# A hybrid decoder layer on one core: three fills ahead of the first attention scores, compressed turns placed later, FFN tiles at fixed homes, tables and gate weights issued later

## The chip, the core and the metric

The kernel runs on one core of a Trainium2 chip. TensorE (PE) multiplies matrices into PSUM, where eight banks of 128 x 512 f32 words hold results; VectorE (DVE), ScalarE (ACT) and GpSimd (POOL) move and change data between PSUM and the on-chip memory SBUF; SyncE (SP) starts most of the DMA transfers. Each engine runs its own instructions in the order in which the program lists them, and waits on semaphores for the others. The metric is the device time of one execution in microseconds.

## The reference

One layer over a sequence of 512 tokens and 1024 channels, all in f32:

```python
h = rmsnorm(x, norm_mix_pre);  z = h @ w_in            # 1024 -> all projections
y_rnn  = rg_lru(causal_conv(xr)) * gelu(gr)            # recurrent branch
kc_c, vc_c = compress(kc), compress(vc)                # MLPs over blocks of 32 tokens
o = g0 * attn(q, kc_c, vc_c) + g1 * attn(q, k_sel, v_sel) + g2 * attn(q, k_win, v_win)
y = sigmoid(gm_rnn) * y_rnn + sigmoid(gm_attn) * o
x = x + rmsnorm(y @ w_out, norm_mix_post)
gate, up = split(rmsnorm(x, norm_ffn_pre) @ ffn_w_gate_up)
x = x + rmsnorm((silu(gate) * up) @ ffn_w_down, norm_ffn_post)
x = x + sigmoid(x @ ple_w_gate + ple_b_gate) * (p @ ple_w_proj)
```

There are 16 query heads in 4 key groups, 64 channels per head. The attention has three branches: over compressed keys (31 blocks), over selected blocks (with 8 blocks and a choice of up to 16, all are selected) and over a window of 512 tokens. Scores carry a bias that falls with distance (ALiBi).

## The kernel before, in words

**Arithmetic.** A product in full precision is three matmuls: each f32 operand is split into a high part and a low part (hi = rounded copy, lo = value - hi), and PE sums hi·hi, hi·lo and lo·hi. So weights that arrive by DMA (`raw`) are cast by ScalarE (`wh`) and subtracted by VectorE (`wl`), and activations that leave PSUM take the same two steps (`aTh` and `aTl`, `PT`, `pc`).

**Stages.** Norm and the value projections come first (up to about 40 us of the profile), then the recurrent branch and the compress MLPs (to 180), the attention (to 468), the output projection and the second norm (to 530), the FFN's gate and up products in 22 column blocks (to 748), its down product (to 860), and the gated embedding, here the tail (to 924).

**The attention's order.** The 16 heads go in 8 pairs, each in two halves of the queries, `run(p, 0, ...)` and `run(p, 1, ...)`. The order of PE's work in a run is a string, in which a letter is a step and a digit is a number of fills. S makes a block of scores (`scores`; VectorE evicts it with the bias at L837, ScalarE takes the exponential at L840). T is a turn: it transposes probabilities (`turn_step`, PE L99) and splits them into hi and lo (`PT`, ScalarE L922, VectorE L923). M multiplies them with the values. X, Y and Z are the compressed branch of the group after this one: its scores, its softmax (which ends on POOL, L888) and its turn, four transposes and the split `pc` (ScalarE L902, VectorE L904). C multiplies `pc` with the compressed values. Y's last steps scale by the gates. A fill is one step of the other projections that the layer needs (three matmuls, one eighth of the inputs of a 128 x 512 block); it keeps PE at work while the others evict. All fills come from one list, so a fill moved ahead is the same work earlier. Ahead of the first run stand the first pair's own scores, with fills between them in the numbers of `PRO`; the first group's X, Y and Z stand there too. PSUM banks are shared by name: two each for `mm` (fills), `sc` (scores) and `tr` (turns), one each for `pv` and `mq` (products).

**Keys.** The keys of a group are copied to the other half of the partitions by a DMA from POOL's queue (L750), `KS<-KS`; the first scores need them.

**Tables.** POOL builds the distance tables `toep` and `ctab` (iota and a triangular select) and clears `KC`, `Vz` and `vct`. `issue_after(x)` puts what is issued inside it behind instruction x in the program's order. `last["pow"]` is the latest power -1/2 that POOL took for a norm.

**FFN and tail.** The pool `ff` gives tiles by tag in the order of their first use, in memory that other stages have left; a tile that lies on such memory waits for its last reader. In the tail `ple_gate_load` loads 512 KB of gate weights and splits them on ScalarE (L1209) and VectorE (L1210); it runs four times for each half of the columns. `to_T` transposes x into `aTh`/`aTl` (L243, L244), the operand of the tail's product. L1380 to L1383 add the gate's bias, take the sigmoid, multiply and add.

## Time and profile before

| | |
|---|---|
| time, median of 3 runs | 924.7 us (924.44 to 926.46) |
| the profiled execution | 926.09 us, span 924.3 us |
| granted PE clock | 0.999 of full speed |
| PE busy | 903.7 us, 98% of the span |
| VectorE busy | 617.5 us, 67% |
| ScalarE busy | 491.5 us, 53% |
| POOL busy | 128.2 us, 14% |
| chain that ended last | PE 82%, VectorE 9%, ScalarE 4%, DMA 3% |

An engine's busy time is the sum over its instructions, so the rest of the span is time in which it stood still. The chain is the work that ended last, followed back from the last instruction to what released each step. In the timeline a start is a time from the start of the span; consecutive equal instructions stand in one row. The ends of matmuls are modelled, so a hole between two of them is read better from the two starts.

### The profile page before, as it was taken

The page shows a single profiled execution, that of the slowest core. Times are in us where ns is not written, and L with a number is a line of the kernel's source. Part 1 is how long each engine was busy: PE and PEld are TensorE (multiplying, and loading weights), DVE is VectorE, ACT ScalarE, POOL GpSimd, SP SyncE. Part 2 cuts the span into 40 slices and gives each one's busy share as a digit, 9 for nine tenths or more (in the row PEclk, how much of TensorE's full clock was granted, in tenths as well). Part 3 has the DMA queues.
Part 4 walks back from the last instruction along what each step waited for, and adds up shares of the span by engine and source line. Part 5 has one row for each costly group of instructions (what it writes and reads, how often), then busy time and mean ns, then how long its engine had stood idle before and what let it go on. Part 6 is the DMA issues. An engine that isn't in the chain of part 4 may idle for free.

```text
span 924.3 us, 12453 instructions
## 1 busy us (share of the span) xinstructions
PE 903.7 (98%) x4493; PEld 745.3 (81%) x4493; DVE 617.5 (67%) x1205; ACT 491.5 (53%) x898; POOL 128.2 (14%) x211
## 2 busy tenths in 40 slices
PE   7999999999999999999999999999999999999997
PEld 6978888867878878888888988888888888877786
DVE  6657886967788788886857444434333478898932
ACT  6468868656667667666744322223222245465600
POOL 3001202122243213233303000000000000000100
PEclk9999999999999999999999999999999999999999
DMA  9334345462123111201055123333333345626401
GB/s 298 87 91 114 101 118 147 99 106 66 50 60 78 46 47 46 69 30 62 27 200 160 55 83 91 102 104 91 92 104 101 91 138 186 200 93 224 151 35 46
DMA packets 124206, 94.58 MB, mean 102 GB/s; under 512 B 6168, under 2 KB 107376, under 8 KB 124144
## 3 DMA queue, kind: packets, MB, share of 16 engines
q1 hardware_dynamic: 122976, 91.68, 33.6%
q0 software_dynamic: 1152, 2.10, 1.5%
q8 instruction: 35, 0.57, 0.3%
q14 instruction: 27, 0.22, 0.1%
q10 hardware_dynamic: 16, 0.00, 0.0%
HBM read 89.58 MB, written 2.10 MB: 99 GB/s over the span
## 4 chain that ended last, share of the span: by engine, by line
PE 82%; DVE 9%; ACT 4%; DMA 3%; issue 2%; POOL 0%; SPq 0%; POOLq 0%; ACTq 0%; DVEq 0%
PE mm L96 42%; PE sc L96 24%; PE mq L96 5%; PE tr L96 4%; PE tr L99 4%; PE pv L96 4%; DVE wl L158 1%; DVE PT L923 1%; DMA x<-in_x_dram 1%; DMA KS<-KS 1%; DMA raw<-in_ple_w_gate_dram 1%; DVE aTl L1210 1%; DVE e L837 1%; ACT e L840 1%; DVE T L1222 1%
## 5 line engine op out<-in xcount | busy, mean ns | idle before, releaser
L96 PE MATMUL mm<-aTh,wh 128*128 128x512 f32 (+1 forms) x536 | 211.6, 395 | 0.6 <-ACT st L1157 0.6
L96 PE MATMUL mm<-aTl,wh 128*128 128x512 f32 (+1 forms) x536 | 206.1, 384 | 0.1
L96 PE MATMUL mm<-aTh,wl 128*128 128x512 f32 (+1 forms) x536 | 206.1, 384 | 0.0
L96 PEld LDWEIGHTS mm<-aTh,wl 128*128 128x128 f32 x536 | 100.7, 188 | 20.7
L96 PEld LDWEIGHTS mm<-aTh,wh 128*128 128x128 f32 x536 | 100.9, 188 | 20.2 <-issue 3.4
L84 ACT CAST wh<-raw 128x1024 fp32r<-128x1024 f32 x43 | 45.3, 1054 | 134.4 <-PE mm L96 58.3
L96 PEld LDWEIGHTS mm<-aTl,wh 128*128 128x128 f32 x536 | 101.0, 188 | 16.4 <-DVE aTl L244 0.5
L852 POOL TENSOR_SCALAR e<-e,sm 128x128 f32<-128x128 f32 (+3 forms) x128 | 79.2, 635 | 158.2 <-DVE sm L848 120.0
L85 DVE TENSOR_TENSOR wl<-raw,wh 128x1024 fp32r<-128x1024 f32 x43 | 52.6, 1224 | 67.3 <-ACT wh L84 62.7
L158 DVE TENSOR_TENSOR wl<-raw,wh 128x1024 fp32r<-128x1024 f32 x59 | 73.2, 1244 | 28.9 <-ACT wh L157 24.3
L840 ACT ACTIVATE e<-e,mn 128x128 f32<-128x128 f32 (+3 forms) x128 | 71.5, 560 | 31.3 <-DVE mn L837 20.4
L96 PE MATMUL sc<-aTh,wl 128*128 128x512 f32 (+1 forms) x208 | 79.3, 381 | 0.5 <-DVE wl L158 0.5
L96 PE MATMUL sc<-aTh,wh 128*128 128x512 f32 (+1 forms) x208 | 79.3, 381 | 0.0
L96 PE MATMUL sc<-aTl,wh 128*128 128x512 f32 (+1 forms) x208 | 79.2, 381 | 0.0
L157 ACT CAST wh<-raw 128x1024 fp32r<-128x1024 f32 x59 | 61.6, 1048 | 25.6 <-PE mm L96 20.9
L837 DVE CUSTOM_DVE_ANT_0 e<-sc,toep 128x128 f32<-128x128 f32 (+3 forms) x128 | 59.4, 482 | 19.2 <-PE sc L96 18.6
L923 DVE TENSOR_TENSOR PT<-tr,PT 128x512 fp32r<-128x512 f32 x96 | 56.6, 595 | 14.0 <-ACT PT L922 13.2
L922 ACT CAST PT<-tr 128x512 fp32r<-128x512 f32 x96 | 47.9, 512 | 24.9 <-PE tr L99 20.9
L1043 POOL TENSOR_TENSOR ss<-ss,ss 128x1 f32<-128x1 f32 x8 | 4.9, 615 | 388.0 <-ACT junk L1031 388.0
L96 PE MATMUL sc<-KS,QS 128*128 128x512 f32 (+2 forms) x192 | 54.3, 365 | 2.8 <-DMA KS<-KS 1.9
L99 PE MATMUL tr<-ident,e 128*128 128x128 f32 x320 | 48.5, 272 | 0.0
L99 PEld LDWEIGHTS tr<-ident,e 128*128 128x128 f32 x320 | 39.9, 140 | 8.8
(365 smaller groups left out, 1747.2 us busy)
## 6 DMA issues: line engine op xcount, KB each, us to landing
raw<-in_w_in_dram SPq DMA_DIRECT2D x48, 512.0 KB, 3.8
raw<-in_ffn_w_gate_up_dram SPq DMA_DIRECT2D x44, 512.0 KB, 3.8
raw<-in_ffn_w_down_dram SPq DMA_DIRECT2D x30, 512.0 KB, 4.3
raw<-in_ple_w_gate_dram SPq DMA_DIRECT2D x8, 512.0 KB, 4.1
x<-in_x_dram SPq DMA_DIRECT2D x7, 512.0 KB, 8.4
raw<-in_w_out_dram SPq DMA_DIRECT2D x6, 512.0 KB
raw<-in_cmp_k_w_dram SPq DMA_DIRECT2D x4, 512.0 KB, 3.7
raw<-in_cmp_v_w_dram SPq DMA_DIRECT2D x4, 512.0 KB, 3.9
```

What stands on the lines that cost most here:

```text
L84: nc.scalar.copy(h, raw)
L85: nc.vector.tensor_sub(l, raw, f32(h))
L96: return pe(nc.tensor.matmul(*args, **kw))
L99: return pe(nc.tensor.transpose(*args))
L157: nc.scalar.copy(h, RAW[n])
L158: nc.vector.tensor_sub(l, RAW[n], f32(h))
L837: nc.vector.tensor_tensor_reduce(e[:, br, :], src, toep[:, 384 - 128 * i:S], SLOPE[h], BIG, op0=OP.add, op1=OP.min, accum_out=mn[:, u, br: ...
L840: tt(nc.scalar.activation(e[:, br, :], e[:, br, :], AF.Exp, scale=-1.0, bias=mn[:, u, br:br + 1], accum_out=sm[:, u, br:br + 1]))
L852: nc.gpsimd.tensor_scalar(ev, ev, sm[:, v, br:br + 1], 1.0, op0=OP.mult, op1=OP.mult)
L922: nc.scalar.copy(P[:, 0, :2 * n], pt[:, :2 * n])
L923: nc.vector.tensor_sub(P[:, 1, :2 * n], pt[:, :2 * n], f32(P[:, 0, :2 * n]))
L1210: nc.vector.tensor_sub(l, x, f32(h))
```

## The change

Five edits. (a) `PRO` goes from 22 fills ahead of the first scores to 25, with one and two fills fewer at two later places, and the first group's turn moves from ahead of the first run into it (`FIRST`, behind the seventh score step). (b) In `ODD`, the order of the second half of pairs 1, 3 and 5, the turn Z moves past two products and the two fills between them. (c) Ahead of the FFN the tags of `ff` are each asked for once in a fixed order; these tiles are never written, they only decide the addresses. (d) POOL's tables and clears are issued behind the last power of the first norm, not behind the first one. (e) The gate weights of the second half are issued behind the last `aTh` and `aTl` of the transposes that stand inside the tail's second product.

```diff
--- before.py
+++ after.py
@@ -26,10 +26,11 @@
 
 
 HALF0 = "S T S 1 S 2 S T 1 S 2 M S T 1 S T 1 S M M 1 M C 3"
+FIRST = "S T S 1 S 2 S T 1 S 2 M S T 1 S Z T 1 S M M 1 M C 3"
 EVEN = "1 T S T 1 C S M T 1 M T 1 S M T T 1 M 1 S T 1 M T 1 M 1 M 3 M"
-ODD = "T T X 1 S M T C S 1 Y M S 1 T T M 1 S T M 1 T 2 T M Z M 2 M 1 M 1"
+ODD = "T T X 1 S M T C S 1 Y M S 1 T T M 1 S T M 1 T 2 T M M 2 M Z 1 M 1"
 LAST = "T O O T 1 C 1 O 1 M O T T O O O M 2 M M T W 4 T 2 M T M 1 T 1 M 1 M"
-PRO = (22, 5, 0, 2, 1, 10)
+PRO = (25, 4, 0, 2, 1, 8)
 TK = (1, 7, 1)
 TV = (12, 7, 8, 11)
 VP = ()
@@ -395,7 +396,6 @@
     tp(pg[:, :KT], g_rows, ident[:KT, :KT])
     kept(nc.vector.tensor_copy(g_col, pg[:, :KT]))
     xn = norm1_halves(x0)
-    pow0 = last["pow"].ins
     keep_warm(6)
     with tc.issue_after(last["xn"].ins):
         vw_first(0, 2, "a")
@@ -460,7 +460,7 @@
 
 
     late_pool = ctx.enter_context(ExitStack())
-    late_pool.enter_context(tc.issue_after(pow0))
+    late_pool.enter_context(tc.issue_after(last["pow"].ins))
     nc.gpsimd.iota(toep, pattern=[[-1, S]], base=384, channel_multiplier=1,
                    allow_small_or_imprecise_dtypes=True)
     nc.gpsimd.affine_select(toep, toep, pattern=[[-1, S]], base=384, channel_multiplier=1,
@@ -505,9 +505,10 @@
     e2 = e2_stack.enter_context(tc.tile_pool(name="e2", bufs=2, reuse_waits="tile"))
 
 
-    nc.gpsimd.memset(KC, 0.0)
-    nc.gpsimd.memset(f32(Vz), 0.0)
-    nc.gpsimd.memset(vct, 0.0)
+    with tc.issue_after(last["pow"].ins):
+        nc.gpsimd.memset(KC, 0.0)
+        nc.gpsimd.memset(f32(Vz), 0.0)
+        nc.gpsimd.memset(vct, 0.0)
     w2src = [a[n_][0].rearrange("(k p) d -> p k d", p=128) for n_ in ("cmp_k_w2", "cmp_v_w2")]
     for u in range(2):
         nc.sync.dma_start(w2k[:, :, u, :], w2src[0])
@@ -969,7 +970,7 @@
         g = p // 2 + 1
         do = {"S": lambda: scores(*next(ss)), "T": lambda: turn_step(p, half, next(ts)),
               "M": lambda: pv_step(p, half, next(ms)), "C": lambda: pv_cmp(p, half), "O": lambda: y_split(next(ys)),
-              "W": lambda: split_out(), "X": lambda: cmp_scores(g), "Y": lambda: cmp_soft(g), "Z": lambda: cmp_turn(g)}
+              "W": lambda: split_out(), "X": lambda: cmp_scores(g), "Y": lambda: cmp_soft(g), "Z": lambda: cmp_turn(g if half else 0)}
         for c in order.replace(" ", ""):
             if c.isdigit():
                 fill(int(c))
@@ -993,9 +994,8 @@
     fill(PRO[4])
     cmp_soft(0)
     fill(PRO[5])
-    cmp_turn(0)
     for p in range(KT - 1):
-        run(p, 0, HALF0)
+        run(p, 0, HALF0 if p else FIRST)
         run(p, 1, (EVEN, ODD)[p % 2])
     p = KT - 1
     run(p, 0, HALF0)
@@ -1187,6 +1187,14 @@
     lateb_stack.close()
     wo_stack.close()
     ff = ctx.enter_context(tc.tile_pool(name="ff", bufs=1, reuse_waits="tile"))
+
+    ff.tile([128, 2, S], F32, tag="st", name=nm("home"), bufs=2)
+    for j in range(NJ2):
+        if j % 2 == 0:
+            n = len(BLK[j // 2])
+            ff.tile([128, n, 4, HS], F32, tag=f"r{j // 2}", name=nm("home"))
+            ff.tile([128, n, 2, HS], F32, tag=f"a{j // 2}", name=nm("home"))
+        ff.tile([128, 2, 2, HS], F32, tag=f"s{j}", name=nm("home"))
     for f in range(2):
         gu_act(f, *first[f][1])
     for f in range(2, NF):
@@ -1363,8 +1371,9 @@
     for ch in range(2):
         for i, t in enumerate(ORDER):
             if ch == 0 and i == 2:
-                for k2 in range(4):
-                    ple_gate_load(1, k2)
+                with tc.issue_after(last["Th"].ins), tc.issue_after(last["Tl"].ins):
+                    for k2 in range(4):
+                        ple_gate_load(1, k2)
             tl = slice(t * 128, (t + 1) * 128)
             pj = bank("tr")
             three(pj, [(pT[0][:, k, tl], pT[1][:, k, tl], WP[ch][0][:, k], WP[ch][1][:, k]) for k in range(2)])
```

**PE in the first run.** `tr<-ident,c` is the compressed turn, `tr<-ident,e` a turn of probabilities, `sc` scores, `mm` a fill. Before, the turn stands between the last fill and the run's first scores:

```order
L96 MATMUL mm_2034<-aTh,wl_1893 128x512
L99 MATMUL tr_2060<-ident,c_2004 128x128 x4
L96 MATMUL sc_2074<-KS_1781,QS_1877 128x384 x2
L99 MATMUL tr_2079<-ident,e_1907 128x128
L99 MATMUL tr_2079<-ident,e_1956 128x128
L99 MATMUL tr_2079<-ident,e_1939 128x128
L99 MATMUL tr_2079<-ident,e_1981 128x128
L96 MATMUL sc_2087<-KS_1781,QS_1877 128x384 x2
```

Now, between the seventh score step of the run and the fourth turn:

```order
L97 MATMUL mm_2099<-aTh,wh_1939 128x512
L97 MATMUL mm_2099<-aTl,wh_1939 128x512
L97 MATMUL mm_2099<-aTh,wl_1940 128x512
L97 MATMUL sc_2169<-KS_1781,QS_1879 128x512 x2
L100 MATMUL tr_2174<-ident,c_2010 128x128 x4
L100 MATMUL tr_2184<-ident,e_1966 128x128
L100 MATMUL tr_2184<-ident,e_1987 128x128
L97 MATMUL mm_2099<-aTh,wh_1939 128x512
```

The turn has moved past seven score steps, three turns, one product and the fills between them. (The line numbers of the changed kernel are higher by one here, and by eight to nine in the tail, since lines were added ahead.)

**PE at the end of pair 1.** `mq<-PT` is a product. Before, the turn (`c_2658`) stands between two products:

```order
L99 MATMUL tr_2761<-ident,e_2490 128x128
L99 MATMUL tr_2761<-ident,e_2525 128x128
L96 MATMUL mq_2586<-PT_2700,V 128x512 x2
L99 MATMUL tr_2769<-ident,c_2658 128x128 x4
L96 MATMUL mq_2586<-PT_2728,V 128x512 x2
```

Now it stands two products and two fills later:

```order
L97 MATMUL mm_2754<-aTh,wl_2482 128x512
L97 MATMUL mq_2586<-PT_2749,V 128x512 x2
L100 MATMUL tr_2783<-ident,c_2658 128x128 x4
L97 MATMUL mm_2754<-aTh,wh_2481 128x512
L97 MATMUL mm_2754<-aTl,wh_2481 128x512
L97 MATMUL mm_2754<-aTh,wl_2482 128x512
L97 MATMUL mq_2586<-PT_2764,V 128x2x128 x2
```

Pairs 3 and 5 have the same order.

**VectorE where the tail begins.** `wg` is the low part of a gate weight, `aTl` the low part of the transposed x, `z` the gate, `x` the residual. Before, a weight split stands ahead of the last norm's x, and others between the `aTl`:

```order
L1210 TENSOR_TENSOR wg_7928<-raw_7925,wg_7927 128x1024
L1047 SCALAR_TENSOR_TENSOR x_5026<-C_7560,rstd_7816,x_5026 128x512
L1047 SCALAR_TENSOR_TENSOR x_5026<-U_7214,rstd_7816,x_5026 128x512
L1380 TENSOR_TENSOR z_7853<-mm_7828,b_g 128x512
L1210 TENSOR_TENSOR wg_7934<-raw_7931,wg_7933 128x1024
L244 TENSOR_TENSOR aTl<-sc_7870,aTh 128x4x128
L1210 TENSOR_TENSOR wg_7940<-raw_7937,wg_7939 128x1024
L1382 TENSOR_TENSOR z_7853<-z_7853,tr_7821 128x512
L244 TENSOR_TENSOR aTl<-sc_7877,aTh 128x4x128
L1383 TENSOR_TENSOR z_7853<-z_7853,x_5027 128x512
L244 TENSOR_TENSOR aTl<-sc_7896,aTh 128x4x128
```

Now:

```order
L1047 SCALAR_TENSOR_TENSOR x_5026<-C_7584,rstd_7840,x_5026 128x512
L1047 SCALAR_TENSOR_TENSOR x_5026<-U_7238,rstd_7840,x_5026 128x512
L1389 TENSOR_TENSOR z_7877<-mm_7852,b_g 128x512
L1391 TENSOR_TENSOR z_7877<-z_7877,tr_7845 128x512
L245 TENSOR_TENSOR aTl<-sc_7894,aTh 128x4x128
L1392 TENSOR_TENSOR z_7877<-z_7877,x_5027 128x512
L245 TENSOR_TENSOR aTl<-sc_7901,aTh 128x4x128
L245 TENSOR_TENSOR aTl<-sc_7920,aTh 128x4x128
L245 TENSOR_TENSOR aTl<-sc_7927,aTh 128x4x128
L1218 TENSOR_TENSOR wg_7952<-raw_7949,wg_7951 128x1024
```

The weight splits stand behind all four `aTl`, and the multiply of `z` by the projection (L1391) now stands ahead of the first `aTl`. On SP the last gate weight load now stands behind the first store of the output.

## Rows read from the trace of the kernel before

**Rows 1.** The list of what PE waits for, summed over the span. Columns: engine, line and tile that wait, what they wait for, then us in total, number of times, longest one.

```profile
PE tr L99 <- POOL c L888: 2.1, 3, 0.8
PE sc L96 <- DMA KS<-KS: 1.9, 1, 1.9
PE tr L99 <- DVE sm L848: 1.6, 1, 1.6
PE sc L99 <- DVE aTl L244: 1.6, 1, 1.6
```

**Rows 2.** The timeline of PE, first head pair, from the last fill before the first scores to the end of the first turn's run. Columns here and in the groups that follow: start and duration in us, engine, line, operation, output<-inputs, shape, count of instructions, and in brackets the idle time before and what ended it.

```profile
191.30 0.39 PE L96 MATMUL mm<-aTh,wl 128*128 128x512 f32 x1
193.62 0.47 PE L96 MATMUL sc<-KS,QS 128*128 128x256 f32 x2 [1.93 <-DMA KS<-KS]
...
208.93 0.39 PE L96 MATMUL mm<-aTh,wl 128*128 128x512 f32 x1
210.12 0.66 PE L99 MATMUL tr<-ident,c 128*128 128x128 f32 x4 [0.81 <-POOL c L888]
210.54 0.60 PE L96 MATMUL sc<-KS,QS 128*128 128x384 f32 x2
...
214.72 0.62 PE L96 MATMUL sc<-KS,QS 128*128 128x384 f32 x2 [0.37 <-DVE mn L837]
...
216.74 0.73 PE L96 MATMUL sc<-KS,QS 128*128 128x512 f32 x2 [0.48 <-DVE mn L837]
...
226.54 0.39 PE L96 MATMUL mm<-aTh,wh 128*128 128x512 f32 x1
```

**Rows 3.** The chain of work that ended last, the one step of it that is the DMA which copies the keys to the other half of the partitions. Columns: start, duration, what.

```profile
185.29 8.19 DMA KS<-KS
```

**Rows 4.** The timelines of POOL and VectorE in the first head pair: the scaling of the compressed probabilities, the first eviction of scores of the run, the split of the third turn's probabilities, and the last work of the run.

```profile
209.02 1.05 POOL L888 TENSOR_TENSOR c<-c,csm 128x512 f32<-128x512 f32 x1 [1.27 <-DVE csm L886]
211.17 0.56 DVE L837 CUSTOM_DVE_ANT_0 e<-sc,toep 128x384 f32<-128x384 f32 x1 [2.30 <-PE sc L96]
...
220.88 0.69 DVE L923 TENSOR_TENSOR PT<-tr,PT 128x512 fp32r<-128x512 f32 x1 [0.28 <-ACT PT L922]
...
228.17 0.85 DVE L953 TENSOR_TENSOR att<-pv,pvt 64x256 f32<-64x256 f32 x2
```

**Rows 5.** The timelines of PE, ScalarE and VectorE around the compressed turn at the end of head pair 1 and the start of pair 2.

```profile
272.60 0.66 PE L99 MATMUL tr<-ident,c 128*128 128x128 f32 x4 [1.61 <-DVE sm L848]
...
278.86 0.51 PE L96 MATMUL sc<-KS,QS 128*128 128x384 f32 x2
273.29 1.17 ACT L902 CAST pc<-tr 64x512 fp32r<-64x512 f32 x2 [1.04 <-PE tr L99]
274.49 1.39 DVE L904 TENSOR_TENSOR pc<-tr,pc 64x512 fp32r<-64x512 f32 x2 [0.46 <-ACT pc L902]
277.14 0.85 DVE L953 TENSOR_TENSOR att<-mq,pvt 64x256 f32<-64x256 f32 x2 [1.25 <-ACT pvt L951]
278.02 0.56 DVE L837 CUSTOM_DVE_ANT_0 e<-sc,toep 128x384 f32<-128x384 f32 x1
```

**Rows 6.** The same at the end of pair 3 and the start of pair 4 (PE twice, VectorE's first eviction).

```profile
337.41 0.66 PE L99 MATMUL tr<-ident,c 128*128 128x128 f32 x4 [0.67 <-POOL c L888]
...
343.67 0.51 PE L96 MATMUL sc<-KS,QS 128*128 128x384 f32 x2
342.85 0.56 DVE L837 CUSTOM_DVE_ANT_0 e<-sc,toep 128x384 f32<-128x384 f32 x1
```

**Rows 7.** The timelines of ScalarE and PE at the first silu of the FFN.

```profile
528.18 1.28 ACT L1157 ACT_TABLE_LOAD   x1
529.96 1.09 ACT L1157 ACTIVATE st<-mm 128x512 f32<-128x512 f32 x2 [0.49 <-PE sc L96]
530.61 0.50 PE L96 MATMUL mm<-aTh,wh 128*128 128x512 f32 x1 [0.57 <-ACT st L1157]
```

**Rows 8.** The timelines of POOL, ScalarE, VectorE and PE where the tail begins, and PE's first product with the gate weights of the second half of the columns (the last row).

```profile
863.87 0.55 POOL L231 TENSOR_TENSOR rstd<-rstd,mhalf 128x1 f32<-128x1 f32 x1 [0.70 <-DVE rstd L230]
866.61 1.46 POOL L231 TENSOR_TENSOR rstd<-rstd,mhalf 128x1 f32<-128x1 f32 x1 [0.70 <-DVE rstd L230]
870.20 1.28 ACT L1381 ACT_TABLE_LOAD   x1 [0.56 <-DVE z L1380]
873.50 0.68 DVE L244 TENSOR_TENSOR aTl<-sc,aTh 128x512 fp32r<-128x512 f32 x1
872.09 0.60 PE L99 MATMUL sc<-ident,x 128*128 128x128 f32 x4
874.24 0.66 PE L99 MATMUL sc<-ident,x 128*128 128x128 f32 x4 [1.56 <-DVE aTl L244]
...
892.20 0.63 PE L96 MATMUL mm<-wg,aTh 128*128 128x512 f32 x2
```

**Rows 9.** VectorE at the start of the kernel, and the step of the chain that is the load of the third tile of x.

```profile
6.38 0.77 DVE L322 TENSOR_SCALAR xn<-x,rstd 128x512 f32<-128x512 f32 x1 [0.74 <-POOL rstd L320]
...
7.14 0.47 DVE L322 TENSOR_SCALAR xn<-x,rstd 128x512 f32<-128x512 f32 x1
...
20.09 2.47 DVE L335 SCALAR_TENSOR_TENSOR xn<-x,rstd,gpre 128x1024 f32<-128x1024 f32 x2
7.62 8.49 DMA x<-in_x_dram
```

## The prediction

> **What bounds the kernel now.** I read the page first for the shares, then the list of what TensorE (PE) waits for, then the chain of waits, and last the timeline of the five places that the change touches. The shares are in the table above: PE is busy 98% of the span, at a granted clock of 0.999, so there is neither a clock to win nor an engine to relieve. What can be won is the time in which PE stands still, about 20.6 us (span less busy time), and it is scattered: the longest entries of the list are 1 to 2 us each, and each has its own releaser [rows 1]. The reader should see in that list that three of the five parts of the change stand where its entries come from: the wait for the keys' DMA (1.9) and one of the three for POOL's L888 (2.1) in the first pair, the other two of these and the one for L848 (1.6) at the turns of pairs 1, 3 and 5, and the wait for L244 (1.6) at the tail. The FFN's homes stand at a shorter wait of 0.57 [rows 7], the tables beside the first norm. The number of matmuls doesn't change. So the whole question is, wait by wait, what is late next.
>
> **First pair: three more fills, turn inside.** Before, the last fill starts at 191.30; the first scores follow at 193.62 after 1.93 of waiting [rows 2], because the shifted keys' DMA, started at 185.29, takes 8.19 us and lands at 193.48 [rows 3]. A fill (three matmuls of 512 columns) is the 0.69 us by which such matmuls follow each other in the rows before 226.54 (three starts 0.23 apart). Three fills are 3 x 0.69 = 2.07 us; they end at 191.53 + 2.07 = 193.60, and the scores can start at 193.62 as before. The three come out of the stretch behind (5 + 10 becomes 4 + 8), so PE's work up to the pair is 2.07 shorter there. The turn (four transposes, 0.42 us until the next matmul) leaves its place at 210.12, and with it the hole in front of it, from 208.93 + 0.23 = 209.16 to 210.12, which is 0.96 by starts (0.81 in the row, whose matmul ends are modelled). The first turn's run, at 210.54 before, then starts at 210.54 - 2.07 - 0.42 - 0.96 = 207.1. From there to the fill at 226.54 it took 16.0 us, of which two score steps lost 0.37 and 0.48 by their rows; a wait in a row is 0.15 short of the hole between starts (0.81 against 0.96 at the turn), so 1.15 together. The work without these is 14.85, and it now contains the turn's 0.42. Two new holes: the turn takes one of the two transpose banks, so the probability turn behind it gets the bank of the turn two fills earlier and must wait until VectorE has split that one (before at 220.88, 0.69 long [rows 4]; that turn would now come 4.2 earlier on PE, while VectorE, which waited only once for PE on the way, comes some 3.6 earlier); I put 0.5 on it and 0.1 on the product after it. The end is 207.1 + 14.85 + 0.42 + 0.6 = 222.97 against 226.54: **3.6 us**. The operand is there in time: POOL's L888 ended at 209.02 + 1.05 = 210.07, and by program order PE reaches the turn only after seven score steps and three other turns, more than 9 us behind the start of the run. The price is VectorE's: the splits of the compressed probabilities (1.39, behind ScalarE's 1.17; the same two lines as in [rows 5]) leave the start of the pair, where they held the first two score evictions up, and stand at its end. VectorE's last work of the run ended at 228.17 + 0.85 = 229.0, 2.5 after PE; the same sum of work from a start 3.5 us earlier ends near 225.1, so it doesn't become the bound. If it does, only the first 2.0 stay; if neither new hole comes, 4.3. Range 2.0 to 4.3.
>
> **Turns two products later (pairs 1, 3, 5).** The moved turn passes a product (0.46, two matmuls 0.23 apart), two fills (1.38) and a product (0.46): 2.3 us of PE's work. The waits were 1.61, 0.67 [rows 5, 6] and 0.66 (the rest of the 2.1 in rows 1 beside the first pair's 0.81), so all three go. But the splits behind the turn come later too, and they stand in ScalarE's and VectorE's queues ahead of the first evictions of the next pair, for which PE's third score step waits. Pair 1: turn at 272.60 - 1.61 + 2.30 = 273.29, ScalarE 1.17 to 274.5, with the queue ahead of it 275.15, VectorE 1.39 to 276.5, the output eviction (277.14 before, 0.85) behind it, so the next pair's first L837 starts at 277.24 and not 278.02, ends 0.56 later, and the third scores start at 277.80 and not at 278.86 [rows 5]: gain 1.06 of 1.61. Pair 3: by the same walk the splits end near 342.2, the first L837 moves from 342.85 to about 343.0, and the third scores, at 343.67 before, start at 343.6 [rows 6]: gain 0.07. Pair 5 has the order of pair 3; by the same steps 0.14. Sum **1.3 us**, with 0 (every wait reappears at the third scores) and 2.9 (none) as ends.
>
> **FFN homes.** They fix addresses only. Before, the first silu at 529.96 had waited 0.49 for a matmul, behind its table load (528.18 + 1.28 = 529.46), and PE's next bank waited 0.57 for it [rows 7]. If the first activation tile no longer lies on the up weights that PE still reads, the silu starts at 529.46 and PE's wait of 0.57 shrinks to about 0.1: **0.5 us**; ends 0 (the table load ends no earlier) and 0.6.
>
> **Tail.** The last transposes wait 1.56 for VectorE's L244 [rows 8], whose second one starts at 873.50 because three weight splits stand in VectorE's queue between the norm and it. Now the four splits stand behind all four L244. But the first L244 now stands behind the multiply by the sigmoid, which waits for a table load of 1.28 and the sigmoid itself; walking the queues, POOL's power taking 0.55, as the one before it, and not the 1.46 that it took beside the splits, then norm, z, table load (869.3), sigmoid, the first L244 starts at 871.84 and the second at 873.04. PE's step at 872.09 comes at 872.58 (0.5 later), that at 874.24 comes at 873.78: **0.5 us**. Ends: 0.5 lost (first step late, second not early) and 1.56. What was hidden before must stay so: the second half's splits now end near 883.5, with the last weight load issued behind the first output store; PE needs them at 892.20 [rows 8], so there are 8 us in hand.
>
> **Tables late.** POOL's tables no longer run beside the first norm, where VectorE's L322 took 0.77 beside them and 0.47 later [rows 9]. That lets PE begin 0.3 to 0.7 earlier, and gives nothing: the x load that starts at 7.62 and takes 8.49 sets the next norm, L335 at 20.09, and PE waits for that a second time [rows 9]. In their new place, from about 20.3 (behind the last power), the tables run beside that L335, 1.24 each. If it were slowed as L322 was (0.77/0.47, so 0.8 on 1.24), PE would lose 0.8. **0 us**, from the x load; ends -0.8 and +0.7.
>
> [...] The rows show that L322 is slower beside the index generation, which only writes. [...]
>
> **The sum.** 3.6 + 1.3 + 0.5 + 0.5 + 0 = 5.9 us off the profiled execution's 926.09, which gives 920.2. That execution was 1.4 above the median of the runs shown, 924.7; waits in it are the same events, so I take the 5.9 off the median: **918.8 us**. On this kernel about 0.2% (1.85 us) is what a measurement can tell from no change.
>
> **The rivals.**
> - *Every wait goes and nothing comes instead.* 1.93 + 0.96 + 1.15 + 2.94 + 0.57 + 1.56 = 9.1 us, 915.6 at the utmost; with any one of the new holes about 916.5. For it: each releaser is short. Against: in pairs 3 and 5 VectorE reaches the next evictions no earlier.
> - *VectorE takes the first pair over.* The moved splits meet the long evictions at the end of the first pair, PE then waits there for score banks, and of that part only the keys' wait (1.9) stays; pairs 3 and 5 give nothing, the tail nothing: 1.9 + 0.3 + 0.5 = 2.7, 922.0. For it: in rows 2 the score steps already waited for L837 twice. Against: VectorE is busy 67% of the span and had 2.30 of nothing to do before its first eviction there [rows 4].
> - *The parts cancel or do not act* (the silu bound by its table load, the new turn's place as bad as the old): within 1.85 of 924.7.
> - *Slower: the last gate weights.* The load issued behind the first output store delays the second half of the tail. It decides only if the splits end after 892.2, that is if the load lands 8 us later than I put it; for a run slower by 1.85 it would have to take the 5.9 gained as well, 8 + 5.9 + 1.85 = 15.8 us late, and then some 927. For it: one queue, a store that waits for VectorE. Against: the store's data are there at about 873.
>
> **How the numbers follow.** Forecast (4.5 to 7 us, 917.7 to 920.2) 0.60; all waits go 0.13; VectorE takes over (1.85 to 4.5 us) 0.17; cancel 0.06; slower 0.04. Range 916.4 to 922.0: it holds the forecast, the first rival up to its utmost, and the second down to its worked case, about 0.83. Faster by over 0.2%: 0.60 + 0.13 + 0.17 = 0.90; within 0.06; slower 0.04.
>
> **What would show it.** In the changed profile: no entry for the keys' DMA in PE's list, and none for L888 or L848; the first pair's last fill 3.6 earlier on the clock than 226.54; a short wait of the third score step in pairs 2, 4 and 6 for L837; the wait for L244 split into two of about 0.5 and 0.3 to 0.7; the matmul after the first silu with 0.1 of waiting; a wait of about 0.2 for L335 near 21.5 as before. Wrong would be: the start of the first pair's scores later than 193.7, a wait for L837 over 1 us inside the first pair, or PE waiting for weights at the second half of the tail.

## The result, and the profile after

The changed kernel took 920.88 us (median of 5 runs, 920.38 to 921.69) beside 925.48 us for the kernel before (5 runs, 924.44 to 929.03). The ratio is 0.9945, with a 95% interval of 0.9924 to 0.9966: faster by 0.55%, which is 3.1 to 7.0 us. The forecast was 918.8, with a range of 916.4 to 922.0. The profiled execution took 920.38 (926.09 before); its span is 918.3, 6.0 less than before.

The page's span, and the busy times of the engines:

```profile
span 918.3 us, 12454 instructions
PE 904.1 (98%) x4493; PEld 745.7 (81%) x4493; DVE 617.8 (67%) x1205; ACT 491.5 (54%) x898; POOL 126.9 (14%) x211
```

PE's busy time is as it was (904.1 against 903.7). What went is time in which PE stood still. The list of PE's waits after the change (total, times, longest), the lines that answer to [rows 1]:

```profile
PE sc L97 <- DVE mn L838: 2.0, 3, 0.7
PE sc L100 <- DVE aTl L245: 0.8, 2, 0.5
PE tr L100 <- DVE PT L924: 0.6, 1, 0.6
PE sc L97 <- DMA KS<-KS: 0.3, 1, 0.3
```

The entries for POOL's L888 and for L848 are gone, and the keys' DMA fell from 1.9 to 0.3. A new entry stands at the top: three waits for L837 (now L838), 2.0 together. So a part of what went has only changed its name. The prediction had said that no entry for the keys' DMA would be left; 0.3 is left in this profile.

PE's timeline in the first pair (the lines that answer to [rows 2]), and POOL's and VectorE's there [rows 4]:

```profile
193.51 0.47 PE L97 MATMUL sc<-KS,QS 128*128 128x256 f32 x2 [0.31 <-DMA KS<-KS]
...
206.92 0.52 PE L97 MATMUL sc<-KS,QS 128*128 128x384 f32 x2
...
216.14 0.60 PE L100 MATMUL tr<-ident,c 128*128 128x128 f32 x4
...
217.32 0.44 PE L100 MATMUL tr<-ident,e 128*128 128x128 f32 x2 [0.58 <-DVE PT L924]
...
223.91 0.60 PE L100 MATMUL tr<-ident,e 128*128 128x128 f32 x4
```

```profile
208.66 1.05 POOL L889 TENSOR_TENSOR c<-c,csm 128x512 f32<-128x512 f32 x1 [1.88 <-DVE csm L887]
...
216.57 0.69 DVE L924 TENSOR_TENSOR PT<-tr,PT 128x512 fp32r<-128x512 f32 x1 [0.66 <-ACT PT L923]
```

The scores begin when they did (193.51, 193.62 before), now with the fills ahead of them; the run begins at 206.92 instead of 210.54. The compressed turn at 216.14 finds an operand that was ready at 209.71. The turn of probabilities behind it waits 0.58 for the bank of the one before.

The end of pair 1 and the start of pair 2 [rows 5], PE and VectorE:

```profile
269.65 0.60 PE L100 MATMUL tr<-ident,c 128*128 128x128 f32 x4
...
274.39 0.62 PE L97 MATMUL sc<-KS,QS 128*128 128x384 f32 x2 [0.66 <-DVE mn L838]
271.49 1.39 DVE L905 TENSOR_TENSOR pc<-tr,pc 64x512 fp32r<-64x512 f32 x2 [0.93 <-ACT pc L903]
272.89 0.85 DVE L954 TENSOR_TENSOR att<-mq,pvt 64x256 f32<-64x256 f32 x2
273.77 0.56 DVE L838 CUSTOM_DVE_ANT_0 e<-sc,toep 128x384 f32<-128x384 f32 x1
```

Read from below: the third score step at 274.39 waits for the eviction at 273.77, which stands in VectorE's queue behind the output (272.89), which stands behind the split of the late turn (271.49).

The first silu [rows 7], and the transposes of the tail with the last weight cast [rows 8]:

```profile
524.32 1.28 ACT L1157 ACT_TABLE_LOAD   x1
525.62 1.09 ACT L1157 ACTIVATE st<-mm 128x512 f32<-128x512 f32 x2
```

```profile
867.51 0.66 PE L100 MATMUL sc<-ident,x 128*128 128x128 f32 x4 [0.26 <-DVE aTl L245]
868.71 0.66 PE L100 MATMUL sc<-ident,x 128*128 128x128 f32 x4 [0.54 <-DVE aTl L245]
875.83 1.05 ACT L1217 CAST wg<-raw 128x1024 fp32r<-128x1024 f32 x1 [2.30 <-DMA raw<-in_ple_w_gate_dram]
```

The silu follows its table load at once (the load ends at 525.60, the silu starts at 525.62). The one wait of 1.56 for L244 is now two of 0.26 and 0.54.

To see where the time went, each matmul's start is set against the start of the same matmul in the profile before, and the median shift of a stretch is taken (us; negative is earlier). Stretches are named by the clock of before: the front; the start of pair 0's second half; ahead of and behind pair 1's moved turn; the end of the attention; the FFN; ahead of the tail; the tail. Every later profile stands in it; the kernels are those of the experiments.

| | 17 to 29 | 229 to 240 | 262 to 271 | 279 to 290 | 440 to 490 | 531 to 700 | 800 to 843 | 895 to 918 |
|---|---|---|---|---|---|---|---|---|
| changed kernel | -0.54 | -3.48 | -3.49 | -4.36 | -3.86 | -4.35 | -4.35 | -5.54 |
| after_again | -0.14 | -3.90 | -3.90 | -4.78 | -4.26 | -4.76 | -4.76 | -5.61 |
| a_first_pair | +0.33 | -3.11 | -3.12 | -3.09 | -3.05 | -3.04 | -3.01 | -2.94 |
| a_fills_only | +0.01 | -0.77 | -0.77 | -0.75 | -0.80 | -0.79 | -0.73 | -0.79 |
| a_turn_only | +0.14 | -1.61 | -1.61 | -1.58 | -1.62 | -1.61 | -1.58 | -1.74 |
| b_odd_only | -0.31 | -0.06 | -0.06 | -0.93 | -0.46 | -0.45 | -0.42 | -0.46 |
| c_homes_only | -0.36 | +1.70 | +1.70 | +1.72 | +1.76 | +1.27 | +1.68 | +1.93 |
| d_tables_only | -0.61 | -0.22 | -0.22 | -0.20 | -0.21 | -0.20 | -0.16 | -0.46 |
| e_gates_only | -0.60 | -1.97 | -1.98 | -1.95 | -1.95 | -1.94 | -1.90 | -2.78 |
| after_old_odd | -0.34 | -3.86 | -3.87 | -3.88 | -3.89 | -4.39 | -4.39 | -4.17 |
| odd_earlier | +0.17 | -3.34 | -3.34 | -4.67 | -5.08 | -5.57 | -5.57 | -6.10 |
| further | -0.01 | -3.77 | -3.77 | -5.10 | -5.53 | -6.02 | -5.99 | -6.45 |
| two_fills_fewer | -0.14 | +3.87 | +3.87 | +3.89 | +3.90 | +3.88 | +3.88 | +3.89 |

A step from one column to the next is what happened between them.

### The profile page after: what moved, and what is told of

It reads as the page before. It is cut to its first block, busy times and chain, and to the rows that moved or that the text cites. A ratio compares the mean times of both kernels' runs of the same rounds, so it can differ in the third digit from the quotient of the medians.

```text
span 918.3 us, 12454 instructions
## 1 busy us (share of the span) xinstructions
PE 904.1 (98%) x4493; PEld 745.7 (81%) x4493; DVE 617.8 (67%) x1205; ACT 491.5 (54%) x898; POOL 126.9 (14%) x211
## 4 chain that ended last, share of the span: by engine, by line
PE 83%; DVE 7%; ACT 4%; DMA 3%; issue 1%; SPq 0%; POOL 0%; POOLq 0%; ACTq 0%; DVEq 0%
PE mm L97 43%; PE sc L97 23%; PE mq L97 5%; PE tr L97 4%; PE tr L100 4%; PE pv L97 4%; DMA KS<-KS 1%; DVE wl L159 1%; DMA x<-in_x_dram 1%; DMA raw<-in_ple_w_gate_dram 1%; ACT e L841 1%; DVE aTl L1218 1%; DVE PT L924 1%; DVE e L838 1%; DVE T L1230 1%
## 5 line engine op out<-in xcount | busy, mean ns | idle before, releaser
L158 ACT CAST wh<-raw 128x1024 fp32r<-128x1024 f32 x59 | 61.7, 1049 | 28.1 <-PE mm L97 24.6
L838 DVE CUSTOM_DVE_ANT_0 e<-sc,toep 128x128 f32<-128x128 f32 (+3 forms) x128 | 59.4, 483 | 17.9 <-PE sc L97 17.2
```

Source lines behind the costliest of these rows:

```text
L158: nc.scalar.copy(h, RAW[n])
L838: nc.vector.tensor_tensor_reduce(e[:, br, :], src, toep[:, 384 - 128 * i:S], SLOPE[h], BIG, op0=OP.add, op1=OP.min, accum_out=mn[:, u, br: ...
```

## The experiments

**The first pair: both halves, and each alone.** The edits of the first pair's order, alone in the kernel before:

```diff
-PRO = (22, 5, 0, 2, 1, 10)
+PRO = (25, 4, 0, 2, 1, 8)
...
-    cmp_turn(0)
...
-        run(p, 0, HALF0)
+        run(p, 0, HALF0 if p else FIRST)
```

> The kernel before with the first edit alone: three more fills ahead of the first scores and the first compressed turn inside the first run. My theory (3.6 us, nearly all of the changed kernel's gain, comes from this edit): the first turn of pair 0's second half, at 227.23 before, starts at about 223.6 to 223.9; time 3.3 to 3.6 us below the kernel before. Rival (the moved splits load VectorE and the score evictions wait): a shift of no more than 2.0 at that turn, with waits for L837 over 1 us inside the first run.

Measured: 921.91 us beside 924.88, ratio 0.9965 (0.9951 to 0.9978); the shift at the first turn of the second half is -2.96, with its front 0.33 later than before. Both are 0.3 to 0.6 short of what I had expected, but this is most of the whole change's gain, and no wait for L837 is left in the first run.

The fills alone (the `PRO` line, without the turn):

> The kernel before with the three fills ahead of the first scores, the turn left ahead of the first run. My theory (the two halves of the edit need each other): the wait for the keys' DMA (1.9) goes, but TensorE reaches the compressed turn about 2 us earlier while POOL's L888, which ended at 210.07, comes at most 0.5 earlier, so the wait for L888 grows from 0.8 to 2.2 to 2.8 and the shift behind it is 0.1 to 0.6 us. Rival (the waits are independent): the shift is 1.9 us.

PE's wait list and the turn in its timeline:

```profile
PE tr L99 <- POOL c L888: 3.7, 3, 2.3
...
209.37 0.66 PE L99 MATMUL tr<-ident,c 128*128 128x128 f32 x4 [2.33 <-POOL c L888]
```

Measured: ratio 1.0007 (0.9998 to 1.0016), shift -0.77. The wait for the keys is gone, and the wait for L888 at the turn grew from 0.81 to 2.33: most of what the fills gave, the turn took. The eleven runs do not even show the 0.77 that is left. Seven of them have a granted clock of 0.997 or 0.998, the profiled one 0.999, so a fall of the clock that this profile does not have may have taken it; that is open.

The turn alone (`FIRST`, with `PRO` as before):

> The kernel before with the turn moved into the first run, the fills as before (22, 5, 0, 2, 1, 10). My theory: the wait for the keys' DMA stays at 1.9; the hole at the turn (0.96) and the two waits for L837 (1.15) go, two small ones come (0.6): shift of 1.3 to 1.7 us at the first turn of the second half, so that fills alone and turn alone together give less than the whole edit. Rival (independent waits): 1.7 with the fills' 1.9 making up the 3.6.

```profile
193.29 0.48 PE L97 MATMUL sc<-KS,QS 128*128 128x256 f32 x2 [1.42 <-DMA KS<-KS]
```

Measured: ratio 0.9997 (0.9987 to 1.0008), shift -1.61, with the wait for the keys still there (1.42; their DMA took 7.68 in this execution, 8.19 before). 0.77 and 1.61 make 2.4, the whole edit 3.1 (3.3 to 3.9 in the five other profiles that have both halves): each half needs the other. The medians say the same: the fills alone are 0.7 slower, the turn alone is 0.7 faster, both together are 3.0 faster.

**The late turns of pairs 1, 3 and 5.**

```diff
-ODD = "T T X 1 S M T C S 1 Y M S 1 T T M 1 S T M 1 T 2 T M Z M 2 M 1 M 1"
+ODD = "T T X 1 S M T C S 1 Y M S 1 T T M 1 S T M 1 T 2 T M M 2 M Z 1 M 1"
```

> The kernel before with the turns of pairs 1, 3 and 5 moved two products later, nothing else. My theory: no wait at the three turns, but one for L837 of 0.5 to 0.7 at the third score step of pairs 2, 4 and 6; net 0.9 to 1.1 us at pair 2, 0 to 0.15 at pairs 4 and 6, 1.0 to 1.3 us in all. Rival (the waits simply go): 2.9 us.

Measured: ratio 1.0000 (0.9991 to 1.0009). By the table the turn of pair 1 gives 0.87 (-0.06 to -0.93), and pairs 2 to 6 take 0.47 back: 0.4 in all, under both expectations. Where pair 2 takes back is seen in this kernel's VectorE and POOL rows (the first two) and the kernel before's (the last):

```profile
290.31 1.53 DVE L158 TENSOR_TENSOR wl<-raw,wh 128x1024 fp32r<-128x1024 f32 x1
...
289.41 1.36 POOL L852 TENSOR_SCALAR e<-e,sm 128x512 f32<-128x512 f32 x2 [0.20 <-ACT pvt L951]
...
291.36 1.23 DVE L158 TENSOR_TENSOR wl<-raw,wh 128x1024 fp32r<-128x1024 f32 x1
```

The weight split of 1.23 took 1.53; it now begins at 290.31, 0.46 before the end of POOL's scaling (290.77). A product 3 us later waits for what stands behind it on VectorE, and 0.16 is lost there; at pair 4 the same split goes from 1.43 to 1.63, and 0.2 is lost. In the attention of this profile the five splits that began with 0.24 to 0.56 us of a scaling left to run took 1.31 to 1.63, the longer the more was left. Six others that met a scaling took 1.21 or 1.22, as with POOL idle; there it was the scaling that took longer, 1.40 to 2.17 instead of 0.48 to 0.69. So in each of these eleven meetings one of the two took longer than it does alone.

The opposite, the changed kernel with the old `ODD`:

> The changed kernel with the turns of pairs 1, 3 and 5 at their old place. My theory (that part is worth 0.4 and not 1.3): TensorE's shift from pair 1's turn to the end of the attention is lost by 0.3 to 0.5 against the changed kernel, with waits of 1.6, 0.7 and 0.7 at the turns again; time within 0.8 of the changed kernel. Rival (1.3 as forecast): 1.0 to 1.5 slower.

Measured: 921.59 us, ratio 0.9956 (0.9944 to 0.9969). From 262 to 490 it moves by 0.02 where the changed kernel moves by 0.37: the part is worth 0.4, twice over. The rest of its distance came ahead of the tail, where a product waited for a weight split:

```profile
PE pv L97 <- DVE w L1218: 0.8, 1, 0.8
```

**Homes, tables and gate weights, each alone.**

```diff
+    ff.tile([128, 2, S], F32, tag="st", name=nm("home"), bufs=2)
...
```

> The kernel before with the FFN tiles at fixed homes alone. My theory: the first silu follows its table load at once, TensorE's wait of 0.57 behind it goes, and all later matmuls are 0.4 to 0.5 us earlier than ahead of the FFN; nothing more. Rival (the changed kernel's further gain of 0.57 near 845, where a weight split had held up a product, comes from the new addresses too): a second step of 0.5 to 0.6 us there, against matmuls of 830.

Measured: ratio 0.9999 (0.9985 to 1.0013); at the FFN the shift goes from +1.76 to +1.27, so 0.49, and there is no second step. The +1.70 that it brings from the first pair is the subject of the last section. In the down product 0.4 is lost again, which no other profile shows. There a weight load of PE (PEld) waits for a split, which stands in a VectorE queue that had waited 2.55 for the DMA of a down weight (0.98 before):

```profile
790.08 1.22 DVE L1230 TENSOR_TENSOR T<-raw,T 128x1024 f32<-128x1024 f32 x1 [2.55 <-DMA raw<-in_ffn_w_down_dram]
...
801.89 0.19 PEld L96 LDWEIGHTS pv<-aTl,p 128*128 128x128 f32 x1 [0.48 <-DVE aTl L1218]
```

Whether the new addresses delay that DMA is open; the changed kernel's two profiles, with the same homes, lose nothing there. The wait list of c_homes_only also answers for the weights ahead of the tail:

```profile
PE pv L96 <- DVE w L1218: 0.7, 1, 0.7
```

> The kernel before with POOL's tables and clears behind the last power, nothing else. The changed kernel was 0.54 us earlier between 17 and 185 us, where I had put 0; four kernels with the tables at their old place were -0.30, +0.01, +0.14 and +0.33 there, so chance has about 0.3 us in it. My theory (the x load sets the front, and its duration varies): between -0.4 and +0.4 there, and nothing of it left behind the first scores, which wait for the keys' DMA. Rival (the tables' place gives it): -0.5 or less there, together with a first L322 of 0.47 to 0.49 and the x load landing at 15.6 or earlier.

```profile
6.05 0.49 DVE L322 TENSOR_SCALAR xn<-x,rstd 128x512 f32<-128x512 f32 x1 [0.74 <-POOL rstd L320]
...
19.47 2.83 DVE L335 SCALAR_TENSOR_TENSOR xn<-x,rstd,gpre 128x1024 f32<-128x1024 f32 x2
```

Measured: ratio 0.9993 (0.9981 to 1.0004). The front is 0.61 earlier, which is outside what I had expected of chance, and the rival's conditions are met (L322 takes 0.49, and the x load lands at 15.40). But e_gates_only, with the tables at their old place, had -0.60, with its x load landing at 15.51. In every profile the front's shift is the shift of that landing (16.11 in the profile before) to 0.02 us, save in this one, where a landing 0.71 earlier gave 0.61. The landings lie between 15.51 and 16.44 with the tables at the old place and between 15.40 and 16.29 with them at the new one. So the x load sets the front, and the tables do not.

```diff
-                for k2 in range(4):
-                    ple_gate_load(1, k2)
+                with tc.issue_after(last["Th"].ins), tc.issue_after(last["Tl"].ins):
+                    for k2 in range(4):
+                        ple_gate_load(1, k2)
```

> The kernel before with the second half's gate weights behind the transposes, nothing else. My theory: the transposes that came at 872.09 come 0.3 to 0.5 later, those at 874.24 come 0.4 to 0.7 earlier, and all after them by as much. Rival (the gain in the changed kernel was the earlier weights near 845): 0 behind the transposes. In either case no wait for weights at the second half.

```profile
870.26 0.66 PE L99 MATMUL sc<-ident,x 128*128 128x128 f32 x4 [0.21 <-DVE aTl L244]
871.46 0.66 PE L99 MATMUL sc<-ident,x 128*128 128x128 f32 x4 [0.54 <-DVE aTl L244]
```

Measured: ratio 0.9995 (0.9979 to 1.0010); the shift goes from -1.90 to -2.78 over the tail's start, of which 0.3 is a shorter wait for a weight split (0.2 instead of 0.5), so about 0.6 is the edit's. Its early start of 1.97 is the keys' DMA again: it landed earlier, and the first scores waited 0.57.

**The changed kernel once more.**

> The changed kernel once more, beside the kernels of this series. My theory (its gain was 5.5 in TensorE's clock, of which about 0.5 each came from the x load and from the last weights, by chance): 920.3 to 921.7, ratio to the kernel before 0.9945 to 0.9965; between 17 and 185 us its shift against the profile before is not -0.54 again but anywhere between -0.6 and +0.4. Rival (the front's gain belongs to the change): -0.5 or less there once more.

Measured: 920.64 us (920.32 to 921.33), ratio 0.9951 (0.9937 to 0.9966); the front at -0.14. The front's gain did not come again, as the x load landed at 15.98: it belongs to the load and not to the change.

**Versions that go on from it.** The late turn one product earlier:

```diff
-ODD = "T T X 1 S M T C S 1 Y M S 1 T T M 1 S T M 1 T 2 T M M 2 M Z 1 M 1"
+ODD = "T T X 1 S M T C S 1 Y M S 1 T T M 1 S T M 1 T 2 T M M 2 Z M 1 M 1"
```

> The changed kernel with the turns of pairs 1, 3 and 5 one product earlier (ahead of the third of the moved products, behind the two fills), nothing else. My theory (the late turn's splits are what holds the next pair's evictions): 0.45 us at each of pairs 2, 4 and 6, 1.3 to 1.4 in TensorE's clock behind them, time 0.9 to 1.5 below the changed kernel. Rival (VectorE takes it back behind the pair): under 0.5.

```profile
PE sc L97 <- DVE mn L838: 0.7, 3, 0.2
```

Measured: 919.85 us, ratio 0.9939 (0.9925 to 0.9954). Against the changed kernel the shift grows by 0.45, 0.46 and 0.46 at the three turns, 1.37 in all: the three waits fell from 2.0 to 0.7, and the operand was still in time. In time it is 0.8 below after_again, which ran beside it, where I had expected 0.9 to 1.5; the two intervals overlap. With a 26th fill and the first turn's neighbours parted by a fill:

```diff
-PRO = (25, 4, 0, 2, 1, 8)
+PRO = (26, 4, 0, 2, 1, 7)
...
-FIRST = "S T S 1 S 2 S T 1 S 2 M S T 1 S Z T 1 S M M 1 M C 3"
+FIRST = "S T S 1 S 2 S T 1 S 2 M S T 1 S Z 1 T S M M 1 M C 3"
```

> The changed kernel, carried on by what its trace shows: the turn of pairs 1, 3 and 5 one product earlier (behind two products and two fills, ahead of the third), the first turn's fill put between it and the next probability turn, and a 26th fill ahead of the first scores (7 instead of 8 behind). My theory (what waits now is VectorE's queue behind the late turn, 0.66, 0.70 and 0.66, the transpose bank, 0.58, and the keys, 0.31): each of the three waits falls by 0.46, the bank's wait goes, 1.2 to 2.2 us faster than the changed kernel, about 919. Rival (the compressed operand is late again, or VectorE takes the time back behind the pair): within 0.5 us of the changed kernel.

Measured: 919.14 us (918.50 to 919.48, 6 runs), ratio 0.9925 (0.9908 to 0.9942): 0.75% below the kernel before, the fastest of all, and 1.7 below the changed kernel's median. The wait for the bank went, but a new one of 0.36 for L837 came among the scores ahead of the first run, and the shift behind the first pair (-3.77) lies among those of the kernels with 25 fills. So what its profile shows to be gained is the earlier late turn.

**Two fills fewer**, to lengthen the hole ahead of the first scores:

```diff
-PRO = (22, 5, 0, 2, 1, 10)
+PRO = (20, 6, 0, 2, 1, 11)
```

> The kernel before with two fills fewer ahead of the first scores (20, 6, 0, 2, 1, 11), so that TensorE stands still some 1.4 us longer there, 3 to 3.8 us in all. One kernel with a wait of 2.44 had a granted clock of 0.64 and 0.50 in the 3.6 us behind it and lost 1.57 us, two with 2.1 and 2.33 had none. My theory (the longer the hole, the surer the drop): the drop is there in the profile, matmuls of 512 columns follow each other by 0.43 for some microseconds behind the first scores, 1.5 to 3 us are lost against the kernel before in the end, of which 0.4 to 0.5 without any drop (1.4 more waiting, less the hole of 0.96 at the turn), and the runs' median lies 1 to 2.5 us above it. Rival (the drop was chance and has nothing to do with the hole): full clock, 0.4 to 0.6 us lost.

PE's first scores, the granted clock behind them (the windows view: stretch, its length, busy times of PE, its weight loads, VectorE, ScalarE and POOL with their counts, then granted clock, DMA share and GB/s), and a further wait:

```profile
193.32 0.47 PE L96 MATMUL sc<-KS,QS 128*128 128x256 f32 x2 [3.09 <-DMA KS<-KS]
...
203.10 1.07 PE L96 MATMUL sc<-QS,KC 128*32 128x512 f32 x8 [1.50 <-DVE mn L837]
```

```profile
193.30:195.00 1.70, 1.68 (x6) 1.46 (x7) 0.51 (x4) 0.83 (x4) 0.00 (x0) 0.67 1.01 172
195.00:197.00 2.00, 2.00 (x6) 1.52 (x6) 0.00 (x0) 0.05 (x1) 0.00 (x0) 0.50 0.09 25
197.00:199.00 2.00, 2.00 (x10) 1.60 (x9) 0.00 (x0) 0.32 (x1) 0.00 (x0) 0.93 0.00 0
```

Measured: 929.41 us, ratio 1.0045 (1.0030 to 1.0060), shift +3.9, more than expected. The clock's part is 1.59: from the first scores to the second, with six fills between them, it is 6.03, where the profile before has 3.75 with five fills, and a sixth would make it 4.44. Another 1.50 is a wait for L837 that I had not seen coming, at the compressed scores: a weight split (L158, 199.76) that stood behind the evictions before now stands ahead of them in VectorE's queue. The rest is the 1.38 of work moved behind the hole, less some 0.7 that the earlier DMA and a shorter wait at the turn gave.

## Why the prediction was right, and where it was not

**First pair, forecast 3.6.** The steps came as worked out. The scores begin at 193.51 (193.62 said), the run at 206.92 (207.1 said), the waits for L837 in the run and the hole at the turn are gone, and the new hole at the transpose bank is 0.58 (0.5 said). At the fill of 226.54 the shift is 3.3 in the changed kernel, 3.0 with this edit alone, 3.9 in after_again: the 3.6 lies in the middle. What spreads them is how PE's arrival and the DMA's landing fall in each execution, and the product behind the new hole, which waited 0.27 and 0.28 in the first two (0.1 said) and not in after_again. By the medians the edit alone gave 3.0. (Without the two new holes the prediction's sum gives 4.2, not 4.3.) VectorE did not become the bound.

**Late turns, forecast 1.3: this is the term that was mis-sized, by 0.9.** The words were "gain 1.06 of 1.61" at pair 1, "gain 0.07" at pair 3 and 0.14 at pair 5. The mechanism was right (no wait at the turns, three waits of 0.66, 0.70 and 0.66 for L837 instead), and pair 1 gave 0.87. But the walk stopped at the third score step. VectorE runs on: pairs 3 and 5 gave nothing and lost 0.04 to 0.09 each, and behind pairs 2 and 4 the weight split beside POOL took 0.2 each time. Net 0.4, by b_odd_only and by after_old_odd alike. There is also a slip in the walk at pair 1: 276.5 and 0.85 make 277.35, not 277.24. It did no harm, since the splits came 0.15 earlier than said and the eviction at 273.77, which is 277.26 on the clock of before.

**Homes, forecast 0.5:** 0.49, at the place named. **Tail, forecast 0.5:** from 850 to the tail the changed kernel gained 0.6, and e_gates_only as much. No weight was late: the last split ends at 878.1, and PE needed it at 892.20 less 5.5.

```profile
876.91 1.23 DVE L1218 TENSOR_TENSOR wg<-raw,wg 128x1024 fp32r<-128x1024 f32 x1 [0.65 <-ACT wg L1217]
```

**Tables, forecast 0:** 0, and for the reason given, the x load. Fronts with the tables at their old place lay between -0.60 and +0.33 of the profile before, those with the new between -0.61 and +0.17. In their new place the tables lie beside L335:

```profile
19.76 0.56 POOL L464 IOTA toep<- 128x512 f32 x1
...
20.49 0.81 POOL L466 TENSOR_SCALAR_AFFINE_SELECT toep<-toep 128x512 f32<-128x512 f32 x1
...
19.55 2.82 DVE L336 SCALAR_TENSOR_TENSOR xn<-x,rstd,gpre 128x1024 f32<-128x1024 f32 x2
...
20.97 1.06 PE L100 MATMUL tr<-ident,xn 128*128 128x128 f32 x8 [0.27 <-DVE xn L336]
```

The pair of L335 takes 2.82 and took 2.47 [rows 9], but PE's transposes of the first of them begin 1.42 behind its start, as before (21.51 less 20.09): it is the second one, beside the selects, that grew, and PE does not wait for it. The lower end of -0.8 was therefore no danger, though no row had shown beforehand that 0 was to be taken and not this end. The first L335 ran beside the index generation (from 19.76), and PE's start behind it kept its 1.42; the second ran beside the selects and took longer. But the first had begun 0.21 before POOL, so these rows alone do not tell whether the difference lies in what POOL ran or in the order. Rows of the kernel before have the order alike: POOL runs a select, later a clear, and VectorE two equal splits:

```profile
7.26 0.82 POOL L466 TENSOR_SCALAR_AFFINE_SELECT toep<-toep 128x512 f32<-128x512 f32 x1
8.75 0.95 POOL L509 MEMSET Vz<- 128x1024 f32 x1
...
7.53 1.09 DVE L290 TENSOR_TENSOR VWl<-raw,VWh 128x512 fp32r<-128x512 f32 x1
...
9.07 0.67 DVE L290 TENSOR_TENSOR VWl<-raw,VWh 128x512 fp32r<-128x512 f32 x1
```

Both splits began while the POOL instruction ran, 0.27 and 0.32 behind its start. The one beside the select took 1.09, the one beside the clear 0.67; in the changed kernel, with POOL idle, both take 0.68. So the split beside the select was 0.41 longer and the one beside the clear was not; why the two differ is not shown. The prediction spoke of the index generation alone and passed over the selects, beside which L335 did lose 0.35.

**The sum.** By its span the profiled execution was 6.0 below the one before, by its time 5.7, where I had said 5.9. That the two nearly meet is partly luck, for the span's 6.0 has other terms: 0.9 less from the late turns, 0.5 more from a product ahead of the tail that did not wait, 0.46 more behind the last matmul. The product did not wait in either profile of the changed kernel and waited 0.2 to 0.8 in all the others, so whether this is chance is open. The 0.46 stands in every profile that has the moved turn and in no other: from the last matmul's end to the end of the span they take 4.8 instead of 5.2. Why is open, and 0.3 of it does not reach the time, which lies 2.0 to 2.1 above the span in those kernels and 1.7 to 1.9 in the others.

In the medians the gain is 4.1 to 4.6, and by the parts run alone 3.2 by the ratio (first pair) and under 0.7 for each of the others. So there the forecast was too much by 1.3 to 1.8. Of that 0.9 is the late turns'; the rest lies within the noise of some 0.15%. A likely part of it, which no run shows, is the step from the profile to the median, "waits in it are the same events": the profile before is 1.2 above the medians of the later series, and the wait for the keys, 1.93 in it, was between 0.57 and 2.44 in the other profiles with 22 fills. The forecast of 918.8 was 2.1 too low; 1.3 of this is the gain, and 0.8 is that the kernel before had a median of 925.48 beside the changed one and not 924.7.

**The rivals.** Not all waits went; VectorE did take the late turns' part, which the second rival had among its conditions, but not the first pair; the gate weights were never near.

## What to carry to other kernels

When two waits lie one behind the other, removing the first only brings the engine to the second sooner (0.77 and 1.61 apart, 3.1 together): move the second consumer in the same edit. When a step is moved later to spare its own wait, walk on along the evicting engine's queue to the next pair's work, since the first place at which its own wait is gone need not be the best: of the two places tried, the earlier one, where the operand was still in time, gave 1.4 more. Still earlier ones were not tried.

## What the runs showed of the hardware

In two profiles a hole in PE's work cost more than its length, since the granted clock was lower behind it: in two_fills_fewer, above (1.59 behind a wait of 3.09), and in c_homes_only. There the first scores waited 2.44 for the keys, and the granted clock fell to 0.64 and then 0.50 of full speed behind it; windows as above:

```profile
193.76 0.47 PE L96 MATMUL sc<-KS,QS 128*128 128x256 f32 x2 [2.44 <-DMA KS<-KS]
...
194.78 0.63 PE L96 MATMUL mm<-aTh,wl 128*128 128x512 f32 x1
195.21 0.63 PE L96 MATMUL mm<-aTh,wh 128*128 128x512 f32 x1
```

```profile
193.70:195.50 1.80, 1.74 (x6) 1.48 (x7) 0.51 (x4) 0.88 (x4) 0.00 (x0) 0.64 0.37 94
195.50:197.30 1.80, 1.80 (x5) 1.36 (x5) 0.00 (x0) 0.00 (x0) 0.00 (x0) 0.50 0.00 0
```

Matmuls that follow each other by 0.23 did so by 0.43, and 1.57 us were lost by 197.7; that is why its shift is +1.70 behind the first pair. The profile before (1.93), b_odd_only (2.1) and d_tables_only (2.33) kept full clock over their holes (1.00 from 193 to 201 in the profile before), two_fills_fewer (3.09) did not (0.67, 0.50 and 0.93). With three or four fills more the hole was at most 0.31, and in all seven profiles of such kernels the clock stayed full there (1.00 from 193 to 201 in the changed kernel's). I had not priced this. What it is worth over many runs is not shown. The changed kernel's ten runs lie between 920.32 and 921.69, while 29 runs of the kernel before beside the second series lie between 923.9 and 928.41. The three slowest of these have a mean granted clock of 0.997 or 0.998, and fourteen of the fifteen under 925 have 0.999 or 1.0 (one has 0.948), which fits the drop. But where in a run the clock fell is on record for the profiled ones alone: it is also lower behind the last matmul (0.58 of full speed from 922 us to the end in the profile before, 0.61 from 916 in the changed kernel's), in d_tables_only, whose profile has a mean of 0.998, it was lower from 11.5 to 14.9 us, and odd_earlier, which had no hole there in its profile, has a run of 921.27 with a mean of 0.996.

The keys' DMA itself took between 6.72 (a_first_pair) and 8.70 us (c_homes_only), the same bytes each time. It does not go with the number of fills ahead: 6.83 to 8.70 with 22 of them, 6.72 to 8.61 with 25.
